# Head-wise sums of squares on TensorE: sixteen-pass products with four columns, or row sums in four column quarters and one turn

## The chip, the core and the metric

The kernel runs on one core of a Trainium2 chip. The metric is the time of one execution on the device in microseconds (us), as the median of several runs. The names of the engines are those of the profile: PE is TensorE (its matmuls) and PEld its weight loads, DVE is VectorE, ACT is ScalarE, POOL is GpSimd, SP is SyncE, which here issues DMAs.

## What is computed

The program is a two-layer decoder trunk on 1024 tokens of width 1024. The first layer is a sparse attention: an indexer scores all keys for each query, the 256 best are kept, and sixteen query heads in four groups attend over them. The second layer is a gated short convolution. A gated feed-forward net follows each. The change lies in the normalisation of queries and keys ahead of the rotary embedding:

```python
def _rmsnorm(x, g):
    xf = x.astype(jnp.float32)
    y = xf * lax.rsqrt(jnp.mean(xf * xf, axis=-1, keepdims=True) + NORM_EPS)
    return (y * g.astype(jnp.float32)).astype(x.dtype)
...
    proj = h @ w_in
...
    q = _rope(_rmsnorm(q, q_norm_g), positions)
    k = _rope(_rmsnorm(k, k_norm_g), positions)
```

For each of 16 query heads and 4 key heads, and each token, the mean of 64 squares is needed.

## The kernel before

**Stages.** The times are those of the profiled execution. Until about 100 us the input is transposed and normalised and the conditioning vector is applied. `project` (line 1077) then makes the attention's projections, to about 290 us: first the indexer's, then keys (one call of `rope_pair` for each half of the tokens), then queries (four groups of heads by two halves), then values. Attention follows (`attend`, line 1371), block of 128 queries by block, to about 590 us, and with it, from block 4 on, the output projection. The rest is two feed-forward nets and the convolution.

**rope_pair** (line 1166) handles four heads by 512 tokens. It is called ten times with sums of squares: twice for keys, eight times for queries. For the first and the second rotary half it makes one product with `gemm_tile` (line 822): 128 rows (four heads by 32 dimensions) by 512 tokens. Each product has 8 steps over the depth by 3 matmuls, because operands are split in a high and a low part (`whi`, `wlo`, `hhi`, `hlo`). ACT takes the product out of PSUM twice: scaled by the norm's gain as tile `rt`, and squared as tile `qsq`. Then the squares are summed over each head's 32 rows of both tiles: for each of four blocks of 128 tokens, and for each of the two tiles, a matmul has the squares as its weights (128x128) and the matrix `blk4` (128x4, ones where row and head agree) as its moving operand. The eight results land with tokens on the partitions in 16 columns of one PSUM bank, and DVE copies them to `ssk` (keys) or `ssq` (queries). `rotate` then turns the pair on DVE. `rsqrt_small` makes the factors: for keys after each half, for queries once after the last group (`qsc`, `qsn`).

**Operands are float32** in these sums. The profile shows each such matmul as two weight loads and two matmul passes, so 80 matmuls appear as 160.

**What fills the other engines meanwhile.** The 256 best keys of a query block are found by 31 steps of a binary search (`select`, line 1304). Each step counts, for two blocks of queries, the scores above a threshold (tile `junk`) and moves the threshold with three small operations on DVE (tile `bs`). Blocks 4 and 5 (640 and 768 wide) are counted on DVE; blocks 2 and 3 (384 and 512) and blocks 6 and 7 (896 and 1024) on ACT. When a search ends, `selected` makes a mask (tile `bias`) from it on DVE, and attention on that block needs the mask. During attention DVE also accumulates the later conditioning vectors from rows of `ada_w` (tile `adacc`).

**The order of the work.** The Python code doesn't issue instructions; it records them with a priority (`plan.pri`) and their dependences. `Plan.drain` (line 501) then runs a model of the engines with fixed costs (`cost`, `CHANGE`, the rate given to `matmuls`) and emits each engine's instructions in the order in which the model would start them. Every engine works through its own list strictly in order. So a changed cost or operation in one place moves other instructions, also in later stages. `plan.copy` may be put on ACT or on DVE. A call of `matmuls` is one piece for the planner; matmuls recorded singly can be placed apart. `form` is the shape in which a piece uses the array; `CHANGE` is what the planner charges for passing from one form to another.

Of the kernel before, what the change touches and what calls it, by code (L numbers as in the profile page):

```python
# [9 lines left out]
F32 = mybir.dt.float32  # L10
# [175 lines left out]
class Plan:  # L186
# [3 lines left out]
    SLACK = (0.3, 0.1, 0.1, 0.1, 0.0)  # L190
    WINDOW = 3.41
    BIAS = 0.8
    ROWS, COLS, PARTS = (64, 128), (128, 64), (64, 128, 2)
    CHANGE = {(ROWS, None): 0.285, (None, ROWS): 0.115, (None, COLS): 0.12, (COLS, None): 0.15,
              (ROWS, COLS): 0.277, (COLS, ROWS): 0.278,
              (PARTS, None): 0.1, (None, PARTS): 0.115, (PARTS, COLS): 0.105,
              (COLS, PARTS): 0.148}
    TRAIL = 1.0 / 450e3
    SPAN, SHAKE = 100, ()
    TABLES, SWITCH = (AF.Silu, AF.Sin, AF.Exp), 1.28  # L200
# [89 lines left out]

        return self.record("vector", "tensor_tensor", (out, a, b), {"op": op})

    def matmuls(self, calls, rate, start=True, stop=True, form=None):

        n = len(calls)
        emits = [self.emitter("tensor", "matmul", c, {"start": start and i < 2,
                                                      "stop": stop and i >= n - 2})
                 for i, c in enumerate(calls)]

        def emit():  # L300
            for e in emits:
                e()

        op = Op("tensor", rate * calls[0][0].free, emit, self.rank())
        op.form = form or tuple(calls[0][1].shape)
        outs = [c[0] for c in calls]
        self.note(op, [r for c in calls for r in c], outs)
        return op
# [253 lines left out]
P = 128  # L562
# [31 lines left out]
def blk(b):  # L594
    return slice(b * P, (b + 1) * P)


class Trunk:
# [111 lines left out]
    def setup(self, cz, c, positions, ada_b, n1, n2, conv_w, gq, gk, lg, lb, rope_c, arenas, kgb, freq):  # L710
        nc, cp = self.nc, self.cp
        self.ident = ident = cp.tile([P, P], F32, name="ident")
        nc.gpsimd.memset(ident, 1.0)
        nc.gpsimd.affine_select(ident, ident, pattern=[[-1, P]], compare_op=ALU.is_equal,
                                fill=0.0, base=0, channel_multiplier=1)
        self.nss = cp.tile([P, 4], F32, name="nss")
        self.blk4 = cp.tile([P, 4], F32, name="blk4")
        nc.vector.memset(self.blk4, 0.0)
        for i in range(4):
            nc.vector.memset(self.blk4[32 * i:32 * i + 32, i:i + 1], 1.0)  # L720
        rc = arenas[0].part_of(0)[0:9, P:2 * P]
        for r0, n, v in ((0, 8, c.rearrange("o (k p) -> (o k) p", p=P)), (8, 1, rope_c)):
            nc.scalar.dma_start(rc[r0:r0 + n, :], v)
        pv = self.ps("mm")
        nc.tensor.transpose(pv[:, 0:9], rc, ident[:9, :9])
        self.cact = cp.tile([P, 8], F32, name="cact")
        nc.scalar.activation(self.cact, pv[:, 0:8], AF.Silu)
        nc.vector.tensor_copy(cz[:, :, 0], self.cact)
        nc.vector.tensor_copy(freq, pv[:, 8:9])
        self.plan.pri = 1.0  # L730
        rows, rowb = arenas[0].part_of(1)[:, 0:P], arenas[1].part_of(0)[0:96, 0:P]
        nc.vector.memset(rows, 0.0)
        for r0, n, v in ((R_N1, 16, n1.rearrange("l (k p) -> (l k) p", p=P)),
                         (R_N2, 16, n2.rearrange("l (k p) -> (l k) p", p=P)),
                         (R_CW, 24, conv_w.rearrange("o w (k p) -> (o w k) p", p=P))):
            nc.sync.dma_start(rows.part_of((1, r0))[r0:r0 + n, :], v)
        nc.sync.dma_start(rowb, ada_b.rearrange("l (k p) -> (l k) p", p=P))
        g = arenas[1].part_of(96)[96:98, 0:HD]
        for r, v in enumerate((gq, gk)):
            nc.sync.dma_start(g[r:r + 1], v)  # L740
        for i, r in enumerate(R_G):
            nc.vector.tensor_copy(
                rows.part_of((1, r))[r:r + 2].rearrange("p (r q) -> p r q", q=32),
                g[:, 32 * i:32 * i + 32].unsqueeze(1).to_broadcast([2, 4, 32]))
        self.vec = vec = cp.tile([P, P], F32, name="vec")
        pv = self.ps("mm")
        read = [1] + [(1, r) for r in (R_N1, R_N2, R_CW, *R_G)]
        nc.tensor.transpose(pv[:, 0:P], rows.part_of(read), ident)
        nc.vector.tensor_copy(vec, pv[:, 0:P])
        self.adab = cp.tile([P, 96], F32, name="adab")  # L750
        pb = self.ps("mm")
        nc.tensor.transpose(pb[:, 0:96], rowb, ident[:96, :96])
        nc.vector.tensor_copy(self.adab, pb[:, 0:96])
        self.plan.pri = 27.0
        self.kgb = kgb.rearrange("p (a d) -> p a d", d=HD)
        for i, v in enumerate((lg, lb)):
            nc.sync.dma_start(self.kgb.part_of(i)[:, i], v.to_broadcast([P, HD]))
        mod = cp.tile([P, 2, 6, 8], F32, name="mod")
        self.mod = [[mod.part_of((i, j))[:, i, j] for j in range(6)] for i in range(2)]
        aff = cp.tile([P, 2, 2, 8], F32, name="aff")  # L760
        self.aff = [[aff.part_of((i, j))[:, i, j] for j in range(2)] for i in range(2)]
# [160 lines left out]
class Attention:  # L922
# [42 lines left out]


    def first_norm(self, x, positions, setup):
        tk, nc, plan, sp = self.tk, self.nc, self.plan, self.pj
        self.C, self.S = (self.hp.tile([P, T], F32, name=v) for v in "CS")
        plan.pri = 0.0  # L970
        cz = self.score[7][:, 0:HW].part_of("c").rearrange("p (k m) -> p k m", m=HD)
        nc.vector.memset(cz, 0.0)
        setup(cz, (self.C, self.S))
        self.kp.tile([P, 32], F32, name="pad")
        xt = [self.kp.tile([P, KT, HW], F32, name="xt%d" % i, tag="k%d" % i) for i in range(NH)]
# [190 lines left out]
    def rope_pair(self, w, half, ts, col, ss, s):  # L1166


        tk, nc, sp = self.tk, self.nc, self.pj
        n = ts.stop - ts.start  # L1170
        ab, sqs = [], []
        for two in range(2):
            self.unit(s)
            ps = tk.gemm_tile(w[two], P, self.h[half], ts=ts)
            t = sp.tile([P, HW], F32, name="rt", tag="rt")[:, 0:n]
            if col is None:
                self.plan.copy(t, ps)
            else:
                c = R_G[two] + col
                nc.scalar.activation(t, ps, AF.Copy, scale=tk.vec[:, c:c + 1])  # L1180
            if ss is not None:
                sq = sp.tile([P, HW], F32, name="qsq", tag="t2")
                nc.scalar.activation(sq, ps, AF.Square)
                sqs.append(sq)
            ab.append(t)
            s += 1
        if ss is not None:
            sm = tk.ps("mm", "sq")[:, 0:16].rearrange("p (t n) -> p t n", n=4)
            for i in range(4):
                for two in range(2):  # L1190
                    nc.tensor.matmul(sm[:, i, :], sqs[two][:, blk(i)], tk.blk4,
                                     start=two == 0, stop=two == 1)
            nc.vector.tensor_copy(ss[:, half * 4:half * 4 + 4, :], sm)
        sl = slice(half * HW + ts.start, (half + 1) * HW)
        tmp = [sp.tile([P, HW], F32, name="sw", tag="sw")[:, 0:n] for _ in range(2)]
        tk.rotate(ab, tmp, self.C[:, sl], self.S[:, sl])
        return ab, sl, s
# [892 lines left out]
```

## Time and profile before

| | us |
|---|---|
| three runs, median | 2259.11 (2258.15 to 2259.2) |
| the profiled execution, its own time | 2256.06 |
| its span in the trace | 2254.3 |
| busy in the span: PE, DVE, ACT | 2201.4, 1901.4, 1137.5 |

The profiled execution lies 3.05 us under the median. Its span is 1.76 us shorter than its time. Views that the prediction uses: windows give the busy time of each engine in a stretch; the chain is the work that ended last, followed backwards; the timeline lists instructions in order with their start and duration (neighbours of one kind are merged and counted, and a matmul's duration includes its latency, so the distance between starts tells the rate); waits say who waited for whom.

### The profile page before, as it was taken

What the parts mean: (1) busy time and instruction counts of PE and PEld (TensorE: products, weight loads), DVE (VectorE), ACT (ScalarE), POOL (GpSimd) and SP (SyncE); (2) the same over time, 40 slices, a digit from 0 to 9 for tenths busy, and PEclk for the clock granted to TensorE, in tenths of its full rate; (3) what the DMA queues carried; (4) which work ended last, traced back from release to release, by engine and by line L of the source; (5) the groups of instructions that cost most, each with busy time, mean ns of one, the idle gap of its engine ahead of it and who ended that gap; (6) DMA issues with size and microseconds to landing.
All of it is one profiled execution on the core that took longest, in us unless ns stands there. A gap on an engine that the chain in (4) does not pass through costs nothing.

```text
span 2254.3 us, 32414 instructions
## 1 busy us (share of the span) xinstructions
PE 2201.4 (98%) x11299; PEld 1770.8 (79%) x11299; DVE 1901.4 (84%) x3892; ACT 1137.5 (50%) x2169; POOL 4.5 (0%) x19
## 2 busy tenths in 40 slices
PE   7999989999999999999999999999999999999999
PEld 4758867777788778888888787877888888888887
DVE  6899999798699899887898998986898877768974
ACT  5478899878564233333445552234553333334444
POOL 0000000000000000000000000000000000000000
PEclk9999989999999999999999999999999999999999
DMA  9403233442365655456972444235446432349824
GB/s 334 119 21 94 85 107 111 127 125 67 113 187 159 205 183 178 157 172 231 389 270 92 142 141 130 90 109 162 124 118 191 151 121 86 123 147 388 283 87 138
DMA packets 332542, 352.68 MB, mean 156 GB/s; under 512 B 20025, under 2 KB 217690, under 8 KB 332378
## 3 DMA queue, kind: packets, MB, share of 16 engines
q1 hardware_dynamic: 332168, 350.48, 48.8%
q8 instruction: 88, 1.44, 0.3%
q14 instruction: 76, 0.62, 0.1%
q10 hardware_dynamic: 210, 0.14, 0.0%
HBM read 278.97 MB, written 68.94 MB: 154 GB/s over the span
## 4 chain that ended last, share of the span: by engine, by line
PE 80%; DVE 8%; issue 6%; ACT 3%; DMA 2%; SPq 0%; ACTq 0%; POOL 0%; POOLq 0%; DVEq 0%
PE ps_g L280 44%; PE ps_mm L280 31%; PE ps_o L280 3%; DVE u L280 2%; PE ps_L L280 2%; DVE wlo L280 1%; DVE s L280 1%; ACT karena L280 1%; DVE v L280 1%; ACT p L280 1%; DMA raw<-in_ada_w_dram 1%; ACT pf L280 1%; DMA raw<-in_ffn_w_gate_dram 1%; ACT junk L280 0%; DMA adaw<-in_ada_w_dram 0%
## 5 line engine op out<-in xcount | busy, mean ns | idle before, releaser
L280 ACT CAST whi<-raw 128x512 fp32r<-128x512 f32 x308 | 190.6, 621 | 398.1 <-PE ps_g L280 152.1
L280 PE MATMUL ps_g<-t,whi 128*128 128x512 f32 x1184 | 367.3, 392 | 3.5 <-ACT whi L280 3.3
L280 ACT CAST whi<-s 128x512 fp32r<-128x512 f32 x276 | 170.9, 621 | 320.3 <-PE ps_g L280 132.1
L280 PE MATMUL ps_g<-h,whi 128*128 128x512 f32 x1056 | 326.3, 390 | 1.4 <-ACT whi L280 1.3
L280 DVE TENSOR_TENSOR wlo<-raw,whi 128x512 fp32r<-128x512 f32 x312 | 214.3, 688 | 80.7 <-ACT whi L280 79.9
L280 PEld LDWEIGHTS ps_g<-t,whi 128*128 128x128 f32 x1184 | 222.8, 189 | 51.3 <-ACT whi L280 5.5
L280 PE MATMUL ps_g<-t,wlo 128*128 128x512 f32 x592 | 232.4, 393 | 3.2 <-DVE wlo L280 3.1
L280 PEld LDWEIGHTS ps_g<-h,whi 128*128 128x128 f32 x1056 | 197.6, 188 | 42.8 <-ACT whi L280 2.3
L280 PE MATMUL ps_g<-h,wlo 128*128 128x512 f32 x528 | 205.7, 390 | 0.5 <-DVE wlo L280 0.5
L280 DVE TENSOR_TENSOR wlo<-s,whi 128x512 fp32r<-128x512 f32 x276 | 188.6, 688 | 15.4 <-ACT whi L280 14.8
L280 PE MATMUL ps_mm<-t,whi 128*128 128x512 f32 x608 | 187.9, 390 | 2.6 <-ACT whi L280 2.5
L280 PE MATMUL ps_g<-ph,whi 128*128 128x512 f32 x572 | 178.4, 389 | 0.0
L280 PEld LDWEIGHTS ps_g<-t,wlo 128*128 128x128 f32 x592 | 111.8, 189 | 30.8 <-DVE wlo L280 7.6
L280 PEld LDWEIGHTS ps_mm<-t,whi 128*128 128x128 f32 x608 | 113.9, 188 | 27.4 <-ACT whi L280 3.9
L280 PEld LDWEIGHTS ps_g<-ph,whi 128*128 128x128 f32 x572 | 107.3, 188 | 22.1
L280 PE MATMUL ps_mm<-t,wlo 128*128 128x512 f32 x304 | 118.8, 391 | 1.7 <-DVE wlo L280 1.6
L280 ACT ACTIVATE junk<-sc,bs 128x896 bf16<-128x896 f32 (+3 forms) x124 | 109.7, 885 | 17.1 <-DVE bs L280 9.7
L280 DVE TENSOR_TENSOR u<-u 128x512 f32<-128x512 f32 x170 | 114.6, 687 | 3.2 <-ACT u L280 2.1
L280 PEld LDWEIGHTS ps_g<-h,wlo 128*128 128x128 f32 x528 | 99.0, 188 | 21.9 <-DVE wlo L280 1.3
L280 PE MATMUL ps_g<-ph,wlo 128*128 128x512 f32 x286 | 110.8, 389 | 0.0
L280 DVE SCALAR_TENSOR_TENSOR adacc<-adaw,cact,adacc 128x512 f32<-128x512 f32 x140 | 104.6, 747 | 6.0 <-DMA adaw<-in_ada_w_dram 5.4
L280 DVE TENSOR_TENSOR s<-raw 128x512 f32<-128x512 f32 x112 | 75.8, 688 | 26.7 <-DMA raw<-in_ffn_w_gate_dram 22.9
(332 smaller groups left out, 4687.2 us busy)
## 6 DMA issues: line engine op xcount, KB each, us to landing
adaw<-in_ada_w_dram SPq DMA_DIRECT2D x160, 256.0 KB, 3.2
ph<-in_ffn_w_down_dram SPq DMA_DIRECT2D x66, 512.0 KB, 6.7
raw<-in_ffn_w_gate_dram SPq DMA_DIRECT2D x54, 512.0 KB, 4.3
raw<-in_ffn_w_up_dram SPq DMA_DIRECT2D x54, 512.0 KB, 4.3
raw<-in_conv_w_in_dram SPq DMA_DIRECT2D x34, 512.0 KB, 4.0
raw<-in_ffn_w_down_dram SPq DMA_DIRECT2D x44, 256.0 KB, 2.7
ph<-in_ffn_w_down_dram SPq DMA_DIRECT2D x44, 256.0 KB, 4.3
raw<-in_attn_w_in_dram SPq DMA_DIRECT2D x18, 512.0 KB, 3.9
```

What stands on the lines that cost most here:

```text
L280: f(*[a.get() if isinstance(a, Ref) else a for a in args], **{k: a.get() if isinstance(a, Ref) else a for k, a in kw.items()})
```

## The change

The matrix `blk4` gets 32 columns, of which four hold ones as before. For each of the eight blocks of squares the operands trade places: `blk4` is now the weight and the squares are the moving operand (128 columns). The result has 32 rows, four of them meaningful, with tokens along the row. The four blocks of tokens go to the four column quarters of the array, so that they land on PSUM partitions 0, 32, 64 and 96; the two tiles are accumulated. The eight are one piece for the planner with a rate and a form of its own (`QUARTS`). Then the 128x128 result is copied to SBUF (into the first `qsq` tile), and one more matmul with this copy as its weights and 16 columns of the identity as the moving operand turns it so that tokens are on the partitions. DVE copies the 16 columns to `ssk` or `ssq` as before. The table `CHANGE` gets entries for the new form.

```diff
-    ROWS, COLS, PARTS = (64, 128), (128, 64), (64, 128, 2)
+    ROWS, COLS, PARTS, QUARTS = (64, 128), (128, 64), (64, 128, 2), (128, 32)
...
+              (COLS, PARTS): 0.148, (None, QUARTS): 0.12, (QUARTS, None): 0.15,
...
-    def matmuls(self, calls, rate, start=True, stop=True, form=None):
+    def matmuls(self, calls, rate, start=True, stop=True, form=None, side=2):
 
         n = len(calls)
-        emits = [self.emitter("tensor", "matmul", c, {"start": start and i < 2,
-                                                      "stop": stop and i >= n - 2})
+        emits = [self.emitter("tensor", "matmul", c, {"start": start and i < side,
+                                                      "stop": stop and i >= n - side})
                  for i, c in enumerate(calls)]
...
-        self.blk4 = cp.tile([P, 4], F32, name="blk4")
+        self.blk4 = cp.tile([P, 32], F32, name="blk4")
...
         if ss is not None:
-            sm = tk.ps("mm", "sq")[:, 0:16].rearrange("p (t n) -> p t n", n=4)
-            for i in range(4):
-                for two in range(2):
-                    nc.tensor.matmul(sm[:, i, :], sqs[two][:, blk(i)], tk.blk4,
-                                     start=two == 0, stop=two == 1)
-            nc.vector.tensor_copy(ss[:, half * 4:half * 4 + 4, :], sm)
+            ps = tk.ps("mm", "sq")
+            self.plan.matmuls([(ps.part_of(g)[32 * g:32 * g + 32, 0:P], tk.blk4, sq[:, blk(g)])
+                               for sq in sqs for g in range(4)], 3.5e-3, side=4)
+            row = sqs[0][:, 0:P]
+            self.plan.copy(row, ps.part_of([0, 1, 2, 3])[:, 0:P])
+            sm = ps.part_of("n")[:, P:P + 16]
+            nc.tensor.matmul(sm, row, tk.ident.rearrange("p (g q) -> p g q", q=32)[:, :, 0:4],
+                             start=True, stop=True)
+            nc.vector.tensor_copy(ss[:, half * 4:half * 4 + 4, :],
+                                  sm.rearrange("p (t n) -> p t n", n=4))
```

Three places of the built order. The first is TensorE in the query projections. `hhi`, `hlo` are the split input, `whi`, `wlo` the split weights; `blk`, `qsq` are the sums. Before, in the fifth of the eight calls for queries:

```order
L280 MATMUL ps_mm<-hhi_261,wlo 128x512
L280 MATMUL ps_mm<-blk_85,qsq 128x4
L280 MATMUL ps_mm<-hhi_262,whi 128x512
...
L280 MATMUL ps_mm<-hhi_262,wlo 128x512
L280 MATMUL ps_mm<-blk_85,qsq 128x4 x7
L280 MATMUL ps_mm<-hhi_262,whi 128x512
```

The same call now (the numbers behind the names are buffers):

```order
L282 MATMUL ps_mm<-hhi_262,wlo 128x512
L282 MATMUL ps_mm<-qsq,blk_85 32x128 x8
L282 MATMUL ps_mm<-hhi_262,whi 128x512
L282 MATMUL ps_mm<-hlo_599,whi 128x512
...
L282 MATMUL ps_mm<-hhi_262,wlo 128x512
L282 MATMUL ps_mm<-ident,qsq 128x16
L282 MATMUL ps_mm<-hhi_262,whi 128x512
```

Before, one of the eight went ahead as soon as the first squares were there, and twelve matmuls later came the other seven. Now the eight stand together; six matmuls of the next product follow, and then the turn.

The second is ACT. `qsq` with 128x512 is the squaring, `junk` the counting of the searches. Before, in the same call:

```order
L280 ACTIVATE rt<-ps_mm,vec 128x512
L280 ACTIVATE qsq<-ps_mm 128x512
L280 ACTIVATE junk_250,bs<-sc_242,bs 128x384
L280 ACTIVATE junk_250,bs<-sc_247,bs 128x1024
L280 CAST whi<-raw 128x512
```

Now, in that call:

```order
L282 ACTIVATE rt<-ps_mm,vec 128x512
L282 ACTIVATE qsq<-ps_mm 128x512
L282 ACTIVATE junk_250,bs<-sc_243,bs 128x512
L282 ACTIVATE junk_250,bs<-sc_246,bs 128x896
L282 COPY qsq<-ps_mm 128x128
L282 ACTIVATE junk_250,bs<-sc_247,bs 128x1024
```

All ten new copies stand on ACT's list, here behind two counts that follow the second squaring.

The third is DVE where attention begins. `p` and `karena` with `bias` are attention's first masked logits; `junk` is the search of blocks 4 and 5. Before, the last counts ahead of attention:

```order
L280 TENSOR_SCALAR junk_249,bs<-sc_244,bs 128x640
L280 SCALAR_TENSOR_TENSOR bs<-bs 128x2
L280 TENSOR_SCALAR bs<-bs 128x2 x2
L280 TENSOR_SCALAR junk_249,bs<-sc_245,bs 128x768
...
L280 SCALAR_TENSOR_TENSOR adacc<-adaw,cact,adacc 128x512
L280 ISA p,mx<-ps_L,bias_224 128x128
```

Now, some rows behind attention's first logits:

```order
L282 ISA karena,mx<-ps_L,bias_224 128x128
L282 ISA mx 128x1
L282 TENSOR_SCALAR junk_249,bs<-sc_244,bs 128x640
...
L282 RECIPROCAL rs<-sums 128x4
L282 TENSOR_SCALAR junk_249,bs<-sc_245,bs 128x768
```

Before, 30 of the 31 steps of this search stood ahead of attention's first logits; now 29 do, and one more stands behind. The searches on ACT move in the same way: 31, 31, 19 and 19 counts (384, 512, 896 and 1024 wide) stood ahead of the first exponential of attention, now 30, 30, 18 and 18. Later stages have the same instructions on every engine, in places in another order.

More of the change, by code (lines that the diff above doesn't have):

```diff
@@ L196 @@
               (PARTS, None): 0.1, (None, PARTS): 0.115, (PARTS, COLS): 0.105,
-              (COLS, PARTS): 0.148}
+              (COLS, PARTS): 0.148, (None, QUARTS): 0.12, (QUARTS, None): 0.15,
+              (ROWS, QUARTS): 0.277, (QUARTS, ROWS): 0.278, (PARTS, QUARTS): 0.105,
+              (QUARTS, PARTS): 0.148, (COLS, QUARTS): 0.15, (QUARTS, COLS): 0.15}
     TRAIL = 1.0 / 450e3
```

## The prediction

> **What bounds the kernel now.** I read the windows first: the projections end and attention begins at about 290 us, and all ten sums lie before that. Columns: stretch, length, then busy time and count of PE, PEld, DVE, ACT, POOL, the granted clock, DMA share and GB/s.
>
> ```profile
> 150.00:175.00 25.00, 22.35 (x100) 13.99 (x100) 24.82 (x51) 13.14 (x25) 1.04 (x2) 1.00 0.00 1
> 175.00:200.00 25.00, 24.41 (x119) 20.26 (x118) 23.38 (x82) 20.96 (x43) 0.00 (x0) 0.93 0.44 127
> 200.00:250.00 50.00, 50.00 (x254) 42.49 (x253) 48.19 (x171) 46.59 (x99) 0.00 (x0) 1.00 0.27 85
> 250.00:290.00 40.00, 40.00 (x281) 37.50 (x281) 38.16 (x148) 34.17 (x77) 0.00 (x0) 1.00 0.40 109
> 290.00:350.00 60.00, 52.65 (x453) 38.12 (x452) 59.29 (x238) 59.65 (x178) 0.00 (x0) 0.86 0.35 101
> 350.00:400.00 50.00, 47.12 (x417) 36.02 (x414) 46.25 (x152) 48.06 (x113) 0.00 (x0) 1.00 0.39 111
> 400.00:450.00 50.00, 50.00 (x413) 39.03 (x413) 37.70 (x134) 44.19 (x92) 0.00 (x0) 1.00 0.41 122
> ```
>
> From 175 to 290 PE is full (114.4 of 115 us), but DVE is nearly so (109.7; 5.3 idle), and ACT has 13.3 us idle. From 290 to 400 ACT (107.7 of 110) and DVE (105.5) are the full ones, and PE has 10.2 us free. From 400 on PE is full again. The chain says who ends last in each (start, length, what):
>
> ```profile
> 180.92 98.50 PE ps_mm L280 x534
> 294.72 3.53 ACT p L280 x15
> 358.62 1.40 DVE s L280
> 395.25 5.67 PE ps_mm L280 x24
> ```
>
> PE holds it from 181 to 279; then pieces of ACT and DVE take turns, of which two are shown, until PE's long pieces come back (395). So time saved on PE in the projections has to pass a stretch of some 100 us in which PE isn't the bound.
>
> **What the old sums cost on PE.** The group as a whole, then one call (the fifth for queries) in the timeline:
>
> ```profile
> L280 PE MATMUL ps_mm<-blk,qsq 128*128 128x4 f32 x160 | 19.3, 242 | 0.0
> ```
>
> ```profile
> 227.35 0.39 PE L280 MATMUL ps_mm<-hlo,whi 128*128 128x512 f32 x1
> 227.58 0.39 PE L280 MATMUL ps_mm<-hhi,wlo 128*128 128x512 f32 x1
> 227.81 0.28 PE L280 MATMUL ps_mm<-blk,qsq 128*128 128x4 f32 x2
> 227.95 0.48 PE L280 MATMUL ps_mm<-hhi,whi 128*128 128x512 f32 x1
> 228.26 0.40 PE L280 MATMUL ps_mm<-hlo,whi 128*128 128x512 f32 x1
> ...
> 230.55 0.39 PE L280 MATMUL ps_mm<-hhi,wlo 128*128 128x512 f32 x1
> 230.78 1.62 PE L280 MATMUL ps_mm<-blk,qsq 128*128 128x4 f32 x14
> 232.25 0.48 PE L280 MATMUL ps_mm<-hhi,whi 128*128 128x512 f32 x1
> 232.57 0.40 PE L280 MATMUL ps_mm<-hlo,whi 128*128 128x512 f32 x1
> ```
>
> A 512-column matmul starts every 0.23 us. Without the two passes at 227.81 the matmul at 228.26 would start at 227.81 + 0.23 = 228.04: they cost 0.22. Without the fourteen at 230.78 the last one would start at 231.01 instead of 232.57: 1.56. One call costs 1.78 us, ten cost 17.8 (the group's 19.3 busy us overlap their neighbours).
>
> **What the new sums cost on PE.** No column quarter runs in this trace. The nearest row is attention's product in column halves, also float32 with 128 moving columns and two passes for each matmul:
>
> ```profile
> 414.06 0.39 PE L280 MATMUL ps_mm<-ohi,wlo 128*128 128x512 f32 x1
> 414.37 1.31 PE L280 MATMUL ps_o<-pf,vst 128*64 128x128 f32 x20
> 415.62 1.30 PE L280 MATMUL ps_L<-ks,qs 64*128 64x128 f32 x12
> ```
>
> ```profile
> 408.71 0.50 PE L280 MATMUL ps_mm<-ohi,whi 128*128 128x512 f32 x1
> 409.04 0.39 PE L280 MATMUL ps_mm<-olo,whi 128*128 128x512 f32 x1
> ```
>
> ```profile
> 333.71 0.88 PE L280 MATMUL ps_o<-pf,vst 128*64 128x128 f32 x12
> 334.51 0.66 PE L280 MATMUL ps_mm<-ident,adacc 128*128 128x128 f32 x4
> ```
>
> Twenty passes take 1.25 us up to the next start, twelve take 0.80: 0.056 for a pass, or 0.11 for a pair that runs side by side, and 0.13 fixed. Entering costs 0.31 - 0.23 = 0.08, leaving 0.33 - 0.23 = 0.10. Sixteen passes with four side by side are 4 x 0.11 + 0.13 + 0.08 + 0.10 = 0.75 us; with two side by side 1.19; one after another 16 x 0.11 + 0.31 = 2.07. I take four, since the halves run as many passes side by side as there are parts, and keep the others as rivals. The turn is two passes with full weights between 512-column matmuls, as at 227.81: 0.22 (16 moving columns for 4). A call then costs 0.97 instead of 1.78. PE gains 0.81 in each, 8.1 in ten.
>
> **How much of that lies on the path.** The two calls for keys lie before 175 us, where DVE is the full one (24.82 of 25): their 1.6 us are hidden under the indexer's scores. The eight for queries gain 8 x 0.81 = 6.5 us of PE where PE is full. About 1 us of it may go to waits for the new copy (rival below), so PE could hand over to attention 5.5 us earlier.
>
> But each engine has its list. What the change adds elsewhere is small: ten copies on ACT. The nearest row is the 256-column copy below, 0.36 us, as upper end; I take 0.25, or 2.5 us in all, against 13.3 idle. DVE's copy of 16 columns stays, and so do all DMAs of keys and queries, which wait for `rotate` and not for the sums. The wider `blk4` and the planner's new numbers have no run time of their own. The detour over the copy lengthens the way to `ssq` by 1 to 2 us after the last call (a copy, a matmul and their hand-overs). The factors `qsn` that come of it start at 277.89, 17 us ahead of attention's first exponential at 294.72, and that hides it.
>
> ```profile
> 277.89 0.22 DVE L280 TENSOR_SCALAR qsn<-qsc 128x128 f32<-128x128 f32 x1
> ```
>
> ```profile
> L280 ACT COPY vst<-ps_mm 128x256 f32<-128x256 f32 x7 | 2.5, 358 | 1.4 <-PE ps_mm L280 1.3
> L280 ACT ACTIVATE junk<-sc,bs 128x896 bf16<-128x896 f32 x18 | 18.7, 1041 | 3.0 <-DVE bs L280 2.7
> L280 ACT ACTIVATE junk<-sc,bs 128x512 bf16<-128x512 f32 x22 | 15.9, 722 | 0.5
> ```
>
> ```profile
> L280 DVE TENSOR_SCALAR_CACHE_REDUCE junk<-sc,bs 128x640 bf16<-128x640 f32 (+1 forms) x52 | 49.0, 943 | 0.3
> L280 DVE DVE_READ_ACCUMULATOR junk<-sc,bs 128x1 f32 x52 | 4.4, 84 | 0.0
> ```
>
> DVE's work doesn't shrink; it is pushed. The order moves one step of the search of blocks 4 and 5 from ahead of attention to behind its start: two counts of 0.94 + 0.08, so 2.05 us, and some small `bs` operations. ACT moves four counts in the same way. That lets attention start earlier, but it is paid back between 290 and 400, where DVE and ACT are full. In total DVE does the same work between 175 and 400, so what arrives at 400 is only the idle time that DVE (or ACT) loses. Which of DVE's idle time hangs on PE is in the waits of 175 to 290 (who waited for whom, total, times, longest):
>
> ```profile
> DVE ks L280 <- ACT ks L280: 1.0, 1, 1.0
> DVE sw L280 <- ACT rt L280: 0.8, 4, 0.2
> DVE bs L280 <- ACT junk L280: 0.8, 3, 0.3
> DVE ssq L280 <- PE ps_mm L280: 0.8, 2, 0.4
> DVE whi L280 <- PE ps_mm L280: 0.4, 1, 0.4
> ```
>
> `sw`, `ssq` and `whi` wait for PE's products directly or through ACT, and `ks` for an ACT operation that follows them: 1.0 + 0.8 + 0.8 + 0.4 = 3.0 us. These go when PE is ahead. I take 3.0 us as the gain that reaches 400 us. From there PE is full, and a shift of its start carries to the end. The other bounds: 0 if DVE waits as long in other places, and 6.5 if DVE's list happens to close all its gaps.
>
> The profiled execution's own time would go from 2256.06 to 2253.1. It lies 3.05 us under the median of the runs, so the same 3.0 us off 2259.11 give **2256.1 us**. I count 0.2% (4.5 us) as about what a measurement of this kernel can tell from no change.
>
> **Rivals.**
>
> *All of PE's gain arrives.* If ACT and DVE between 290 and 400 are full only because they are fed in that order (PE waits there too, and DVE has 3.75 us idle from 350 to 400), all of PE's 6.5 to 8.1 us pass: 2251.0 to 2252.6. For it: PE holds the chain over 98.5 us. Against it: 59.65 and 59.29 of 60 busy us on ACT and DVE right behind.
>
> *The quarters don't run four at once.* The change would not do what it says. With two at a time a call costs 1.19 + 0.22 = 1.41 and gains 0.37; eight gain 3.0 on PE, and if a third arrives it is 2258. If a quarter's weights are loaded only after the passes in the other quarters have ended, the sixteen run one after another: 2.07 + 0.22 = 2.29, a loss of 0.51 in each call, 4.1 on PE in eight, up to 2263. Against both: the halves' 0.056 us for a pass, half of what a pair takes; the second half is not held back by the first. The Trainium skill ("TensorE: Matmul & The Clock Gate", Part 3, what overlaps and what doesn't) has a weight load run beside matmuls in flight only where the row group differs, which is the strict case, since column parts share their rows. The halves here share them too, and by their rate this trace doesn't agree with that rule.
>
> *The turn waits for the copy.* PE works its list in order, so the turn holds up every matmul behind it until ACT has copied. That such a wait occurs on this path is seen once:
>
> ```profile
> 180.92 0.50 PE L280 MATMUL ps_mm<-hhi,whi 128*128 128x512 f32 x1 [0.59 <-ACT qsq L280]
> ```
>
> In the fifth call ACT has counts of 512 and 896 ahead of the copy (0.72 + 1.04 us), PE has six matmuls of 0.23 (1.4 us) between sums and turn. Where ACT reaches the counts only when PE begins the sums, PE waits 1.76 + 0.36 - 1.4 = 0.7, and with ACT one more count behind, 1.7. Above 0.81 for each call it outweighs the gain, and from 1.4 on (8 x 0.6 = 4.8) the kernel is slower by more than a measurement's doubt. At 1.7 eight calls lose 8 x 0.9 = 7 us: 2266. Against it: ACT has 13.3 us idle in that stretch and so is rarely behind, and its counts can start while PE still works on the next product.
>
> **How the numbers follow.** Forecast (part of the gain arrives, 0 to 4.5 us): 0.48. All arrives: 0.27. Quarters two at a time: 0.09; one by one: 0.05. Turn waits: 0.11. The new places of instructions in later stages can shift any of these by a few us either way, since PE still has short waits there. Faster by over 0.2% (under 2254.6): the second case and a part of the first, 0.35. Slower (over 2263.6): the turn's case and an edge of the quarters', 0.12. The rest, 0.53, is no difference. The range runs from 2250.5 (all of the gain) to 2262 (the quarters nearly one by one); outside are the turn's case and the edges.
>
> **What would show it.** In the profile after: sixteen passes of `ps_mm<-qsq,blk` within about 0.6 us from the first start to the next matmul (1.0 if two at a time, 1.9 if one by one); the turn as two passes with 0.22 of cost and no wait for `qsq` by ACT ahead of it; the busy PE total lower by some 8 us; attention's first exponential at about 289 instead of 294; one step of the 640 and 768 counts behind it; DVE's idle time from 175 to 400 lower by 3 of 9.7 us. The forecast is wrong if attention's output products around 395 come 6 us earlier or more, if the turn is named as waiting for ACT by more than 2 us in total, or if the difference arises behind 400 us.

## The result and the profile after

The kernel after takes 2284.77 us (2281.89 to 2285.98), the kernel before in the same comparison 2259.15 us: a ratio of 1.0112, 95% interval 1.0095 to 1.013. It is 25.6 us slower, where 2256.1 was forecast. The profiled executions differ as much: 2281.89 after, 2256.06 before.

**Where the change was made, it did what was forecast.** The timeline of after on PE, in the fifth call for queries (start, duration, what):

```profile
228.34 0.39 PE L282 MATMUL ps_mm<-hhi,wlo 128*128 128x512 f32 x1
228.66 0.64 PE L282 MATMUL ps_mm<-qsq,blk 128*32 128x128 f32 x16
229.24 0.50 PE L282 MATMUL ps_mm<-hhi,whi 128*128 128x512 f32 x1
229.58 0.40 PE L282 MATMUL ps_mm<-hlo,whi 128*128 128x512 f32 x1
...
230.52 0.40 PE L282 MATMUL ps_mm<-hhi,wlo 128*128 128x512 f32 x1
230.75 0.29 PE L282 MATMUL ps_mm<-ident,qsq 128*128 128x16 f32 x2
230.89 0.48 PE L282 MATMUL ps_mm<-hhi,whi 128*128 128x512 f32 x1
231.21 0.40 PE L282 MATMUL ps_mm<-hlo,whi 128*128 128x512 f32 x1
```

The sixteen passes take 0.58 us up to the next matmul. From 228.34 to 229.58 there are two steps of 0.23 without them, so they cost 1.24 - 0.46 = 0.78 us; the turn costs 0.69 - 0.46 = 0.23. That is 1.01 a call where the old sums cost 1.78. The groups by tile name (duration min/median/max in ns, first and last start) show how far this carries; attention's last output product and its first exponential, before and then after:

```profile
L280 PE MATMUL ps_o<-pf,vst x1152: 272/273/477, 298.6 to 586.8; 128*64 128x128 f32 x192
...
L280 ACT ACTIVATE p<-p,nm,qsc x64: 477/878/1254, 294.3 to 560.9; 128x128 f32<-128x128 f32 x8, 128x256 f32<-128x256 f32 x8, 128x384 f32<-128x384 f32 x8, 128x512 f32<-128x512 f32 x8
```

```profile
L282 PE MATMUL ps_o<-pf,vst x1152: 272/273/477, 294.2 to 578.3; 128*64 128x128 f32 x192
...
L282 ACT ACTIVATE p<-p,nm,qsc x64: 478/878/1255, 290.0 to 553.5; 128x128 f32<-128x128 f32 x8, 128x256 f32<-128x256 f32 x8, 128x384 f32<-128x384 f32 x8, 128x512 f32<-128x512 f32 x8
```

Attention begins 4.3 us earlier and its last output product 8.5 us earlier. At 590 us the kernel is ahead.

**Then it loses 34 us in stages that the change does not touch.** The feed-forward product of `t` with `whi` among the groups of before, then PE's busy time and the same product after:

```profile
L280 PE MATMUL ps_g<-t,whi x1184: 387/389/650, 687.7 to 2031.4; 128*128 128x512 f32 x198
```

```profile
PE 2228.1 (98%) x11319; PEld 1761.1 (77%) x11319; DVE 1903.0 (83%) x3888; ACT 1138.9 (50%) x2183; POOL 4.5 (0%) x19
...
L282 PE MATMUL ps_g<-t,whi x1184: 388/394/628, 680.7 to 2053.0; 128*128 128x512 f32 x198
```

The first of these matmuls starts 7.0 us earlier, the last 21.6 us later. Their number is the same, the median of one has gone from 389 to 394 ns, and PE is busy 26.7 us longer (2228.1 against 2201.4) although the sums take less. No wait explains this; PE is as full as before (98%). A stretch in which PE never stops shows the rate itself. Windows from 1700 to 1900 us, PE alone (stretch, length, busy and passes, granted clock, DMA share, GB/s), before and then after:

```profile
1700.00:1900.00 200.00, 200.00 (x884) 1.00 0.47 148
```

```profile
1700.00:1900.00 200.00, 200.00 (x859) 1.00 0.44 140
```

884 passes of 512 columns against 859, at a granted clock of 1.00 both times: one every 226 ns before, every 233 after.

**What differs there.** The matmuls and their number are the same behind 590 us, and so is the granted clock in these windows. Two things are left above all: the planner's new order, and the place of the tiles in SBUF. `blk4` has grown from 4 to 32 float32 columns. In the built programs it takes 128 bytes of a partition instead of 32, and every later tile on the left side of SBUF lies 96 bytes higher. Among these are the moving operands of all later stages (`h`, `t`, `ph`, `rh`, `rt`). The addresses that the built programs assign are these: before, `h` and `t` start at 224 modulo 256 and the weights `whi`, `wlo`, on the right side, at 224 too; after, `h` and `t` start at 64 and the weights still at 224. No trace shows an address; the experiments test what hangs on them by moving tiles by known distances.

### The profile page after: what moved, and what is told of

It is laid out like the page before. It is cut to its first block, busy times and chain, and to the rows that moved or that the text cites. A ratio compares the mean times of both kernels' runs of the same rounds, so it can differ in the third digit from the quotient of the medians.

```text
span 2280.1 us, 32466 instructions
## 1 busy us (share of the span) xinstructions
PE 2228.1 (98%) x11319; PEld 1761.1 (77%) x11319; DVE 1903.0 (83%) x3888; ACT 1138.9 (50%) x2183; POOL 4.5 (0%) x19
## 4 chain that ended last, share of the span: by engine, by line
PE 78%; DVE 9%; issue 6%; ACT 4%; DMA 2%; SPq 0%; ACTq 0%; POOL 0%; POOLq 0%; DVEq 0%
PE ps_g L282 46%; PE ps_mm L282 29%; PE ps_o L282 2%; DVE u L282 1%; DVE s L282 1%; PE ps_L L282 1%; DVE wlo L282 1%; ACT p L282 1%; DMA adaw<-in_ada_w_dram 1%; ACT pf L282 1%; DVE p L282 1%; DVE karena L282 1%; DVE adacc L282 1%; DVE sc L282 1%; ACT karena L282 1%
## 5 line engine op out<-in xcount | busy, mean ns | idle before, releaser
L282 PE MATMUL ps_g<-t,whi 128*128 128x512 f32 x1184 | 373.8, 397 | 1.9 <-ACT whi L282 1.9
L282 PE MATMUL ps_g<-h,whi 128*128 128x512 f32 x1056 | 333.0, 396 | 1.6 <-ACT whi L282 1.6
L282 PE MATMUL ps_mm<-t,whi 128*128 128x512 f32 x608 | 193.0, 397 | 2.1 <-ACT whi L282 2.0
L282 PE MATMUL ps_mm<-ph,whi 128*128 128x512 f32 x308 | 97.7, 394 | 0.0
```

Source lines behind the costliest of these rows:

```text
L282: f(*[a.get() if isinstance(a, Ref) else a for a in args], **{k: a.get() if isinstance(a, Ref) else a for k, a in kw.items()})
```

## The experiments

### Layout alone, and other paddings

The first theory was that the start address of the moving operand counts. The rivals were the new order and the clock. The first kernel is before with the one edit:

```diff
-        self.blk4 = cp.tile([P, 4], F32, name="blk4")
+        self.blk4 = cp.tile([P, 32], F32, name="blk4")[:, 0:4]
```

> The kernel before with one edit: blk4 is allocated with 32 columns instead of 4 and only the first four are used, so no instruction changes, and everything that is allocated behind it on the left side of SBUF lies 96 bytes higher, as in the kernel after. In the profile of after, the 512-column matmuls behind 620 us start 232.8 ns apart instead of 227.0, some 6800 of them, about 40 us in all. Address theory (a 512-column matmul is slower when its moving operand starts on another byte): the whole loss is here, without the gain of 8.5 us that after has by 621 us; after lost 25.6 us in all, so 25.6 + 8.5 = 34 us, 2293 us. Order theory (the plan's new order in the later stages makes PE slower): nothing, 2259 us. Clock theory (the new sums change what the throttle allows later): nothing, 2259 us.

Measured: 2296.63 us, ratio 1.0171 (1.0154 to 1.0188), 37.9 us slower. The order theory and the clock theory fall: this kernel has before's instructions in before's order. Its PE busy time and its window:

```profile
PE 2239.1 (98%) x11299; PEld 1770.8 (77%) x11299; DVE 1907.0 (83%) x3892; ACT 1137.2 (50%) x2169; POOL 4.5 (0%) x19
```

```profile
1700.00:1900.00 200.00, 200.00 (x859) 1.00 0.44 140
```

Before has 11299 passes too, busy for 2201.4 us. Here they are busy 37.7 us longer, which is the whole loss, and the rate is after's. Only passes whose moving operand has moved are slower: behind 590 us the median from start to start is 232 ns for `h`, `t` and `ph` (227 before), and still 227 for the 720 passes whose moving operand is `whi` or `wlo`, on the right side.

Three more paddings. The first is after with

```diff
+        self.blank = cp.tile([P, 8], F32, name="blank")
+        nc.vector.memset(self.blank, 0.0)
```

> The kernel after with one tile of 8 columns (32 bytes a partition) behind blk4, so that what follows lies 128 bytes higher than before, not 96: the moving operands of the later stages start at 32 modulo 64 again, as in before. Address theory, if it is the start modulo 64 that counts: the matmuls behind 620 us are 227 ns apart again, and the 8.5 us won by 621 us arrive, 2250 to 2251 us. If it is the start modulo 128 or more: still slow, about 2285 us. Order theory and clock theory: 2285 us, as after.

Measured: 2277.92 us, ratio 1.0089 (1.0074 to 1.0104). Still slow: not a matter of the start modulo 64. The window:

```profile
1700.00:1900.00 200.00, 200.00 (x862) 1.00 0.45 143
```

Then before with the same two lines, and before with `[P, 16]` in them:

> The kernel before with a tile of 8 columns behind blk4: everything behind it lies 32 bytes higher, and the moving operands of the later stages start at 0 modulo 64. Address theory, start modulo 64: as slow as with 96 bytes, 2293 us. If it is the start modulo 128 or 256 (112 or 224 before, so 0 here): may be either. Order and clock theory: 2259 us.

> The kernel before with a tile of 16 columns behind blk4: everything behind it lies 64 bytes higher, so the moving operands of the later stages start at 32 modulo 64 as in before, but at another place modulo 128. Address theory, start modulo 64: 2259 us, as before. Address theory, start modulo 128 or more: slower, up to 2293 us. Order and clock theory: 2259 us.

Measured: 2295.87 us with 32 bytes, ratio 1.0164 (1.0148 to 1.0179); 2269.18 us with 64 bytes, ratio 1.0048 (1.0033 to 1.0063). The windows, with 32 and then with 64 bytes:

```profile
1700.00:1900.00 200.00, 200.00 (x859) 1.00 0.45 141
```

```profile
1700.00:1900.00 200.00, 200.00 (x875) 1.00 0.46 146
```

So 32 and 96 bytes cost a pass 6.6 ns (200 / 859 against 200 / 884), 128 bytes 5.8 and 64 bytes 2.3. A start modulo 64 or modulo 128 doesn't give this pattern, since after with 32 bytes more keeps before's start modulo both. Only before's own place is fast, where moving operand and weights both start at 224 modulo 256. That gave a new question: does the moving operand's own place count, or its place relative to the weights?

### Moving the weights instead

Before, with 32 bytes put into the weights' pool on the right side:

```diff
+        tk.wp.tile([P, 8], F32, name="blank", tag="blank", bufs=1)
```

> The kernel before with a tile of 8 columns in the pool of the weights on the right side of SBUF: whi, wlo, hhi, hlo, ohi and olo lie 32 bytes lower (192 modulo 256 instead of 224), while the moving operands of the stages behind 620 us (h, t, ph, rh, rt) stay at 224 modulo 256. Own-address theory (a 512-column matmul is slower when the moving operand's own start is not at 224 modulo 256): behind 620 us still 227 ns from start to start; in the projections and in the output product, whose moving operands have moved, about 232 ns, some 460 + 380 matmuls by 5 to 6 ns, so 4 to 5 us: 2263 us. Relation theory (what counts is that moving operand and weights start at the same place modulo 256, as they do in before): the reverse, 227 ns in the projections, about 232 ns behind 620 us, 34 us: 2293 us.

Measured: 2294.92 us, ratio 1.016 (1.0146 to 1.0173), with the order of before. The moving operands of the later stages have not moved by a byte, and the loss is there, 36.3 us:

```profile
1700.00:1900.00 200.00, 200.00 (x859) 1.00 0.44 140
```

In the projections `hhi`, `hlo` and the weights moved together. Their groups, in before and in this kernel (min/median/max in ns), have the same median:

```profile
L280 PE MATMUL ps_mm<-hhi,whi x224: 276/389/628, 44.7 to 265.3; 128*128 128x512 f32 x96, 128*128 128x256 f32 x16
```

```profile
L280 PE MATMUL ps_mm<-hhi,whi x224: 278/389/632, 43.6 to 266.2; 128*128 128x512 f32 x96, 128*128 128x256 f32 x16
```

The own-address theory falls; what counts is the distance between the two.

### The rate by itself

A kernel of nothing but 512-column matmuls, nine moving tiles each 32 bytes further modulo 256 than the last, and the weights in turn at three places:

```python
mv = [pool.tile([P, HW + 8], F32R, name="mv" + v) for v in "abcdefghi"]
...
for p, w in ((ps[1], 0), (ps[2], 24), (ps[3], 32)):
    for m in mv:
        run(p, m, w)          # 24 matmuls, weights wt[:, w:w + 128] and the next 128 in turn
```

> A kernel of 912 matmuls of 512 columns and little else; it leaves out the whole computation of the reference. Moving operands lie in nine tiles, each 32 bytes further modulo 256 than the one ahead (mva at 128, mvb 160, mvc 192, mvd 224, mve 0, mvf 32, mvg 64, mvh 96, mvi 128 again), weights at 128 (psa), 224 (psb) and 0 (psc) modulo 256, with no other engine at work; then psd, weights at 224, while DVE and ACT copy and DMAs write to SBUF. Own-address theory, without contention: mvd is the fastest tile in psa, psb and psc alike (about 227 ns a matmul), mvf about 2 ns slower, the others about 5 to 6 ns. Relation theory: the fastest tile goes with the weights (mva and mvi in psa, mvd in psb, mve in psc). Contention theory (the address counts only because of other engines' accesses to SBUF): all nine alike in psa, psb and psc, and apart only in psd.

The timeline (start, duration, what; a group's length is the distance to the next start):

```profile
17.13 5.60 PE L31 MATMUL psa<-mva,wt 128*128 128x512 f32 x24
22.57 5.77 PE L31 MATMUL psa<-mvb,wt 128*128 128x512 f32 x24
28.17 5.67 PE L31 MATMUL psa<-mvc,wt 128*128 128x512 f32 x24
33.68 5.77 PE L31 MATMUL psa<-mvd,wt 128*128 128x512 f32 x24
...
61.70 5.63 PE L31 MATMUL psa<-mvi,wt 128*128 128x512 f32 x24
67.17 5.78 PE L31 MATMUL psb<-mva,wt 128*128 128x512 f32 x24
...
83.97 5.61 PE L31 MATMUL psb<-mvd,wt 128*128 128x512 f32 x24
89.42 5.77 PE L31 MATMUL psb<-mve,wt 128*128 128x512 f32 x24
...
139.72 5.61 PE L31 MATMUL psc<-mve,wt 128*128 128x512 f32 x24
145.17 5.77 PE L31 MATMUL psc<-mvf,wt 128*128 128x512 f32 x24
...
184.30 5.63 PE L31 MATMUL psd<-mvd,wt 128*128 128x512 f32 x24
189.76 5.77 PE L31 MATMUL psd<-mve,wt 128*128 128x512 f32 x24
```

With the weights at 128 (`psa`) the tile at 128, `mva`, is the fast one: 22.57 - 17.13 = 5.44 us for 24, 227 ns each, and `mvi`, back at 128 modulo 256, takes 5.47. `mvb`, 32 bytes further, takes 5.60, 233 ns; `mvc`, 64 bytes further, 5.51, 230 ns. With the weights at 224 (`psb`) the fast one is `mvd` (5.45), with the weights at 0 (`psc`) it is `mve` (5.45). That is the relation theory. It needs no other engine: `psa` to `psc` run alone, and in `psd`, with DVE, ACT and DMAs at work, `mvd` is again the fast one (5.46). The contention theory falls too. The kernels show the same three rates at the same distances: 226 ns at 0, 229 at 64, 232 to 233 at 32, 96 and 128.

The second such kernel asks which weights count, and for what operands:

```python
run(ps["a"], mv, (wa,)); run(ps["b"], mv, (wb,))
run(ps["c"], mv, (wa, wa, wb, wb))       # weights for the passes in turn
run(ps["d"], mv, (wa,), 256); run(ps["e"], mv, (wb,), 256)
run(ps["f"], mv, (wa,), 128); run(ps["g"], mv, (wb,), 128)
run(ps["a"], bmv, (bwa,)); run(ps["b"], bmv, (bwb,))
```

> A kernel of matmuls alone, which leaves out the whole computation of the reference. The moving operand lies at 224 modulo 256. psa: 512 columns, weights at 224 (wta) all along; psb: weights at 0 (wtb); psc: two passes with wta, two with wtb, in turn. Relation theory: psa 227 ns from start to start, psb 232 to 234. In psc it shows which weights count. If it is the weights that are loaded while a pass runs (those of the pass behind it): a wta pass ahead of a wta pass and a wtb pass ahead of a wta pass take 227 ns, the two ahead of a wtb pass 232 to 234. If it is the pass's own weights: both wta passes 227 ns, both wtb passes 232 to 234. psd and pse: 256 columns with wta and wtb, psf and psg: 128 columns; if a load costs the pass a fixed time, the difference stays some 6 ns, and if it is a share of the pass, it falls to 3 and 1.5 ns. psa and psb with bmv: the same with 2-byte operands, no expectation.

```profile
39.38 11.05 PE L41 MATMUL psa<-mv,wta 128*128 128x512 f32 x48
50.27 11.36 PE L41 MATMUL psb<-mv,wtb 128*128 128x512 f32 x48
...
66.10 0.62 PE L41 MATMUL psc<-mv,wta 128*128 128x512 f32 x2
66.56 0.63 PE L41 MATMUL psc<-mv,wtb 128*128 128x512 f32 x2
...
72.59 5.90 PE L41 MATMUL psd<-mv,wta 128*128 128x256 f32 x48
78.33 5.83 PE L41 MATMUL pse<-mv,wtb 128*128 128x256 f32 x48
84.00 5.47 PE L41 MATMUL psf<-mv,wta 128*128 128x128 f32 x48
89.31 5.52 PE L41 MATMUL psg<-mv,wtb 128*128 128x128 f32 x48
94.67 10.53 PE L41 MATMUL psa<-bmv,bwa 128*128 128x512 bf16 x48
105.04 10.52 PE L41 MATMUL psb<-bmv,bwb 128*128 128x512 bf16 x48
```

`psa` takes 10.89 us for 48 passes, 227 ns each. `psb` takes 11.19, 233 ns each; only the weights' place differs. With 2-byte operands the other weights cost nothing (busy 10.53 and 10.52).

With 256 columns there is no loss either (5.74 us with `wta`, 5.67 with `wtb`), and with 128 next to none (5.31 and 5.36). But these rows don't decide between a fixed time and a share. The weight loads follow each other almost without a gap there (busy time, mean ns, idle time):

```profile
L41 PEld LDWEIGHTS psd<-mv,wta 128*128 128x128 f32 x48 | 5.9, 191 | 0.1
```

In `psa` the loads are idle 1.9 us. Half the columns shorten the 48 passes only from 5.74 to 5.31 us, so the loads may set the pace and cover a slower pass.

In `psc` both expectations failed. A pair there takes about 0.46 us, and the trace's starts, from the third round of four on, follow each other at 224, 235, 232 and 236 ns, over and over: short only between two `wta` passes, long in the three other places, also between a `wtb` pass and the `wta` pass behind it. So neither the pass's own weights nor the next ones alone decide it. How the two reads get in each other's way is open.

### The change without its layout

Both kernels have an unused tile of 128 bytes, `pad`, ahead of `xt0`. The wide `blk4` fits into it, and the 32 bytes of the old one stay reserved, so every other tile is at before's address:

```diff
-        self.blk4 = cp.tile([P, 32], F32, name="blk4")
+        cp.tile([P, 4], F32, name="blank")
...
-        self.kp.tile([P, 32], F32, name="pad")
+        tk.blk4 = self.kp.tile([P, 32], F32, name="blk4")
```

> The kernel after with the 32-column blk4 kept in the 128 bytes of the tile called pad, which lies unused ahead of xt0 in both kernels; the 32 bytes of the old blk4 stay reserved. Same instructions in the same order, and every other tile at its address of before. Address theory: the matmuls behind 620 us are 227 ns apart, and the gain of 8.5 us at 621 us arrives at the end: 2259 - 8.5 = 2250.5 us, 0.4% faster than before. Order theory (the re-planned order behind 620 us has a share in the loss): more than 2253 us.

Measured: 2245.88 us, ratio 0.9944 (0.9931 to 0.9958). It beats both kernels: 12.7 us below before, 38.9 below after. The window:

```profile
1700.00:1900.00 200.00, 200.00 (x884) 1.00 0.42 133
```

The parts add up: layout alone 37.9 slower, change alone 12.7 faster, together 25.2; measured 25.6. The gain is larger than the 8.5 us expected, though. The profiled executions (2247.28 and 2256.06) differ by 8.8 us: before's lies 2.5 us under its median here, the other 1.4 above, so the traces can't show all of the 12.7.

### Does PE's time arrive?

The forecast let 3.0 of 8.1 us arrive. To test that share, the sixteen passes are issued three times in the kernel above:

```diff
-            for e in emits:
+            for e in emits * (3 if side == 4 else 1):
```

> The kernel with blk4 in the pad, in which each call's sixteen passes of the sums are issued three times over (the last ones count), so 32 passes more in each of ten calls and nothing else. After, the sixteen took 0.574 us from the first start to the next matmul, so 32 take about 1.15 us, 11.5 us in all ten calls. Theory that PE time in the projections reaches the end in full: 2245.9 + 11.5 = 2257.4 us. Theory of the forecast (between 290 and 400 us DVE and ACT set the pace, and only 3.0 of 8.1 us arrive): 2245.9 + 11.5 x 0.37 = 2250.1 us. Nothing arrives: 2245.9 us.

Measured: 2256.13 us, 10.3 us more than without; ratio to before 0.9985 (0.9976 to 0.9994). The two were not measured side by side; by the distance of each to before the difference is 12.7 - 3.2 = 9.5. Its timeline in the fifth call for queries:

```profile
233.22 1.52 PE L282 MATMUL ps_mm<-qsq,blk 128*32 128x128 f32 x48
234.67 0.50 PE L282 MATMUL ps_mm<-hhi,whi 128*128 128x512 f32 x1
```

48 passes take 1.45 us where 16 take 0.58, so 0.87 is added in a call, 8.7 in ten and not 11.5: the sixteen's 0.58 holds a fixed part that isn't repeated. The profiled execution is 8.85 us longer (2256.13 against 2247.28). That is all of it, where the forecast's share would let 3.2 arrive. Part of it is chance: in the first call for keys the sums start at 120.71 with single sums and at 121.98 here, 1.3 us late before the first extra pass. The first call for queries (the third call), in the kernel with single sums and then in this one:

```profile
183.55 0.64 PE L282 MATMUL ps_mm<-qsq,blk 128*32 128x128 f32 x16
```

```profile
185.15 1.52 PE L282 MATMUL ps_mm<-qsq,blk 128*32 128x128 f32 x48
```

It is 1.6 us late after the two key calls, which added 1.75: nearly all of those is hidden, as forecast. The spans end 8.8 us apart (2254.4 and 2245.6), so the eight query calls' 7.0 us arrive whole. This is shown for time added within one order.

**The new order has effects of its own.** Windows on PE from the 321st of attention's 1152 output passes to the last one, in before, after, the kernel with `blk4` in the pad, and the one with threefold sums (stretch, length, busy and passes, granted clock, DMA share, GB/s):

```profile
392.87:586.80 193.93, 190.88 (x1790) 1.00 0.34 99
```

```profile
390.30:578.30 188.00, 186.88 (x1789) 1.00 0.35 103
392.59:580.50 187.91, 186.81 (x1788) 1.00 0.36 103
399.73:587.66 187.93, 186.82 (x1789) 1.00 0.36 103
```

The same passes lie between the two marks, up to two records, and none of the sums. All three kernels with the new order need 6 us less for them than before, whatever their sums cost. Before with the wide `blk4`, in the old order, needs 194.25. PE idles 1.1 us there instead of 3.0; the rest of the 6 us is open.

Ahead of the first mark these three kernels lose some 4 to 6 us, by an estimate from the leads. The eight query calls save 8 x 0.77 = 6.2 us of PE, and there after is only 2.6 us ahead of before and the kernel with `blk4` in the pad 0.3. With the sums three times over a call costs 1.01 + 0.87 = 1.88 us, slightly more than before's 1.78, and that kernel is 6.9 us behind. At the last mark they are 8.5 and 6.3 ahead and 0.9 behind. So by then the loss is made up, and the leads are near what the sums themselves save or cost.

**What stays open** is the rest of the gain: 8.7 us by the spans and 12.7 (9.5 to 15.6 by its interval) by the medians. In the profiled executions 2.4 us more arise behind the last output product. With the threefold sums the median is 3.2 us below before's, though the spans (2254.4 and 2254.3) are alike. The new order may give this; no run separates it from the rest.

## Why the prediction was wrong, point by point

- **"The wider `blk4` and the planner's new numbers have no run time of their own."** This is the step that failed: a term put at nothing. The wider `blk4` costs 37.9 us, in a kernel that uses only its four old columns. It costs nothing where it is used; it moves the operands of some 6200 matmuls by 96 bytes against their weights, and each takes some 6 ns more. The prediction costed instructions and looked at their order. It did not ask what a new size in a pool moves. The forecast's own test applied: the difference arises behind 400 us. The range ended at 2262, and the 0.12 for a slower kernel was given to the turn's wait and to slow quarters; neither occurred, so that the kernel is slower was not foreseen by it. PE's busy total, forecast some 8 us lower, is 26.7 higher, and 14.5 lower (2186.9) with `blk4` in the pad.
- **Old sums 1.78 us, new sums 0.75, turn 0.22.** Right: 0.78 and 0.23, so 0.77 a call instead of 0.81, by the fifth call for queries.
- **Four quarters at once.** Right, against the rival: 0.58 us for sixteen passes, forecast about 0.6. The Trainium skill ("TensorE: Matmul & The Clock Gate", Part 3, what overlaps and what doesn't) has weight loads overlap running matmuls only where the row group differs. The quarters share their rows, and this trace does not agree with it: one load takes 0.110 us, and sixteen loads with their passes 0.58.
- **The turn waits for the copy.** It did not. The ten copies after, and the only wait of PE that the trace lists for tile `qsq`, by loads for `ps_L` and not by the turn:

```profile
L282 ACT COPY qsq<-ps_mm x10: 243/252/338, 121.2 to 265.8; 128x128 f32<-128x128 f32 x10
...
  PEld ps_L L282: 0.2, 1
```

  The copy's 0.25 us is as forecast.
- **Attention's first exponential at about 289.** Right: 290.0 after, 289.4 with `blk4` in the pad. Before, it starts at 294.3; the forecast's 294.72 is the start of a piece of the chain.
- **"What arrives at 400 is only the idle time that DVE (or ACT) loses", 3.0 us, and "a shift of its start carries to the end".** The size at 400 was close, the reason and the second half were wrong. At the first mark of the windows above (392.87 us before) after is 2.6 us ahead and the kernel with `blk4` in the pad 0.3, so the 6 us or more that would have spoken against the forecast did not occur there. But the lead isn't carried along: by the last output product it is 8.5 and 6.3, in a stretch where the forecast took PE as full. And DVE's idle time from 175 to 400 hardly changed. The window of after (DVE is the third of the busy times):

```profile
175.00:400.00 225.00, 212.51 (x1571) 168.91 (x1571) 215.61 (x785) 211.17 (x515) 0.00 (x0) 0.95 0.38 104
```

  It is 225 - 215.6 = 9.4 us, before 9.7. That PE's time arrives by the end is shown by the sums issued three times. What held the saving up ahead of 393 us, DVE and ACT or the new order, is not shown.
- **The rival "all of PE's gain arrives", 2251.0 to 2252.6**, comes nearer for the change without its layout: the query calls' saving is there by the last output product. That kernel took 2245.88, 5 to 7 us less than the rival gave, the part left open above.

## What to carry to other kernels

A change of a tile's size is a change of the addresses of all that is allocated behind it: compare the addresses of the matmuls' operands before and after, as one compares the instructions. A loss in stages that a change does not touch, with equal counts and a longer time for each instruction, is a sign of this, and one run with the size changed alone tells it from a new order. For 512-column float32r passes (float32r is the 4-byte type of the split operands) that each load their weights, place moving operand and weights at the same start modulo 256.

## What the runs showed of the hardware

- A 512-column float32r matmul pass takes 227 ns when its moving operand and its weights start at the same byte modulo 256 within the partition, about 230 when the moving operand starts 64 bytes further, and 232 to 234 at the other multiples of 32 tried, with no other engine at work. Each pass had its own weight load. bf16 passes showed no such difference (216 ns at both places). Passes of 256 or 128 columns showed at most 1.3 ns (120 and 118, 111 and 112), with weight loads that left almost no gap. The Trainium skill ("SBUF — State Buffer", Operand start alignment) has an operand start at any multiple of its element size and says that this is about legality and not speed; all starts here are legal, and what they cost in speed is the 6 ns above.
- Sixteen float32 passes in four column quarters, with their weight loads, take 0.58 us, and 48 take 1.45: 0.027 us for each further pass.
